# A two-layer encoder trunk on one core: queries through DRAM, fillers in one stream, other buffers and a vector-engine end

## The chip, the core and the metric

The kernel runs on one core of one Trainium2 chip. The metric is device time in microseconds (us); the median of several runs is compared. Engines: TensorE (PE, its weight loads are PEld), VectorE (DVE), ScalarE (ACT), GpSimd (POOL) and SyncE (SP, which here only issues DMAs).

## The reference

x is 1024 tokens of 1024 channels, mem 256 tokens. Two layers share one form:

```
mem_n = layer_norm(mem)
layer A: u, qm, gate = split(x @ a_w_in, [3072, 512, 2048])
         y_mix = silu(layer_norm(depthwise causal conv, 31 taps, 1536 channels, of (a * sigmoid(g))))
layer B: q, k, v, qi, ki, wi, qm, gate = split(x @ b_w_in, [1536, 128, 128, 512, 64, 8, 512, 2048])
         score = sum over 8 index heads of w * relu(qi . ki); the top 256 admissible keys per token are kept
         y_mix = 12-head attention with one key/value head over those keys, logits - slope * distance
both:    y_mem = 4-head attention of qm over mem_n
         x = layer_norm(4 ** 0.25 * x + (concat(y_mix, y_mem) * silu(gate)) @ w_out)
```

Everything is float32.

## The kernel before, in words

Every product is made of three matmuls on rounded halves: an operand is split into a high part (a copy to fp32r, usually by ACT) and a low part (operand minus high, by DVE or POOL), and hi*hi, hi*lo and lo*hi are summed in PSUM (`project_steps`, L143 to L154, one matmul per step of the generator, 24 for 128 output columns of 512 tokens; `project` runs them through). `load_cols` (L135) fetches the weights of 128 columns with two DMAs on SP and splits them, ACT the high and POOL the low part, or POOL both with `pool_only`. `split_ps` (L167) splits a PSUM result.

The program is written in one order; a planner simulates it and lays out each engine's own queue, which then runs strictly in order. `tc.high_priority(offset=...)` moves work forward or (`low`) back in that order, and `tc.issue_after(ins)` ties matmuls behind an instruction.

**Layer A.** x is loaded in 8 token tiles and transposed on PE into xhi and xlo (`transpose_in`, L238: eight transposes into a two-bank PSUM accumulator of tag acc, of which there are two, then `split_ps`). `rows_load` and `rows_in` (L250 to L264) bring conv weights and norm vectors as rows and transpose them into `chan`. Twelve channel blocks of the conv are made in pairs: `u_pair` (L384) projects gate and value, and `conv_pair` (L414) runs 30 multiply-adds over time shifts on DVE (L429) for each block, in a PSUM accumulator; ACT makes the first step (L419) and copies column 0 at the end (L428). `conv_stat` (L433) subtracts a common shift (the mean of block 0, by PE) and sums d and its square for the norm. DVE's conv runs at low priority beside PE's projections. In between stand `mem_prep` (L270, the memory tokens' norm and transposes, tile mf of tag mp), `head_a` (memory heads: `mem_k`, `mem_v`, `mem_q`, `mem_scores`, `mem_values`), `gate_a`, and `k_b`, `v_b` (layer B's memory keys and values, stored to DRAM). Tag mp has one buffer and is shared by mf, the softmax tile pn and kr. Then the output products (`out_group`, L585) and the norm (`layer_norm`, L195: statistics on DVE, scale on ACT, product with g on POOL, sum with b on DVE).

**Layer B.** *Index stage* (L786 to L806): for each of six token blocks and eight index heads PE makes scores (L794, L795) in one of two PSUM buffers, ACT takes relu (L800), and DVE accumulates (L805). After each step, FILL[b] matmuls of a gate projection are put in as fillers; FREE_GATES gates are used so. *Threshold stage*: DVE and ACT search for each token's 256th largest score bit by bit (`threshold`, L835), then `select` (L896) turns scores into a mask plus distance, on DVE at low priority. Beside it PE runs the remaining gates (`gate_steps`, to DRAM) and the queries of the first two heads (`head_q`, L814: high part by ACT, low part by DVE from PSUM, L824). *Attention* (L1096 to L1109): the sequence is heads 0, 1, memory head 0, heads 2, 3, 4, memory head 1 and so on, 16 in all. A head has four units of two token blocks: `scores` (L951; DVE maximum and subtraction, ACT exponential, POOL scale) and, one unit later, `values` (L981; PE transposes, split, products). `between` puts SHARE fillers after each group of transposes: the query of the next head or memory head, then one late gate; what is left runs at the head's end (L1106). Weights of the fillers are loaded one head ahead. The filler's PSUM tag pj has one buffer here.

**End.** `out_group` four times, the last in token order with `finish_b` (L1131): blocks 0 to 5 by `layer_norm` (block 5 with the last sum on POOL), blocks 6 and 7 by `layer_norm_late` (L201: statistics, L204 and two L207 on DVE, two stores).

Of the kernel before, what the change touches and what calls it, by code (L numbers as in the profile page):

```python
# [64 lines left out]
def trunk(ctx, tc, x, mem, mem_g, mem_b, a_w_in, conv_w, conv_b, ln_g, ln_b,  # L65
# [109 lines left out]
    def ln_moments(src):  # L175

        n = uid()
        st = small.tile([P, 2, 6], F32, tag="bnst", name=f"bnst{n}")
        for i in range(2):
            nc.vector.bn_stats(st[:, i, :], src[:, i * 512:(i + 1) * 512])  # L180
# [20 lines left out]
    def layer_norm_late(dst, src, g, b, o):  # L201

        mean, rs = ln_moments(src)
# [11 lines left out]
    with ExitStack() as actx:  # L215
# [28 lines left out]

        def x_in(t):
            transpose_in(xn[t], t)
# [23 lines left out]
        def mem_prep():  # L270
# [19 lines left out]
        def mem_k(w, h, kv=None, raw=None):  # L290

            pc = load_cols(w, h * P)
            o = psum()
            project(pc, mhi, mlo, 0, NMEM, o[:, :NMEM])
            if raw is None:
                split_ps(kv[:, 0:256], kv[:, 512:768], o[:, :NMEM])
            else:
                nc.scalar.activation(raw[:, 0:256], o[:, :NMEM], AF.Copy)

        def mem_v(w, h, kv=None, raw=None):  # L300
# [11 lines left out]
            else:  # L312
                nc.scalar.activation(raw[:, 256:512], o[:, :NMEM], AF.Copy)
# [20 lines left out]
        def mem_scores(pl, tags, q, kv, hf, banks_s):  # L334
# [4 lines left out]
            pn = pl.tile([P, 4, NMEM], F32, tag=tags["p"][hf], bufs=1, name=f"mp{n}")  # L339
# [18 lines left out]
            for i in range(4):  # L358
                nc.gpsimd.tensor_scalar(pn[:, i, :], pn[:, i, :], sm[:, i:i + 1], 1.0, op0=OP.mult, op1=OP.mult)
# [24 lines left out]
        def u_pair(i, start=False):  # L384
# [29 lines left out]
        def conv_pair(hs, i0):  # L414

            accs = []
            for i, h in zip((i0, i0 + 1), hs):
                acc = psb.tile([P, T], F32, tag="acc", bufs=2, name=f"acc{i}")
                nc.scalar.activation(acc, h, AF.Identity, bias=chan[:, i, TAPS:TAPS + 1], scale=chan[:, i, TAPS - 1:TAPS])  # L419
                accs.append(acc)  # L420
            for s in range(TAPS - 1, 0, -1):
                for i, h, acc in zip((i0, i0 + 1), hs, accs):
                    w = chan[:, i, TAPS - 1 - s:TAPS - s]
                    if s > 1:
                        dst = acc
                    else:
                        conv_out[i] = dst = co_tile(f"co{i}")
                        nc.scalar.activation(dst[:, 0:1], acc[:, 0:1], AF.Copy)  # L428
                    nc.vector.scalar_tensor_tensor(dst[:, s:], h[:, :T - s], w, acc[:, s:], op0=OP.mult, op1=OP.add)  # L429
# [3 lines left out]
        def conv_stat(i):  # L433

            d = conv_out[i]
            if i == 0:
                o = psb.tile([P, T], F32, tag="acc", bufs=2, name="cmean")
                for hf in range(2):
                    hs = slice(hf * 512, (hf + 1) * 512)
                    nc.tensor.matmul(o[:, hs], ones, d[:, hs], start=True, stop=True)  # L440
                    nc.scalar.activation(c_sh[:, hs], o[:, hs], AF.Copy, scale=1.0 / P)
            nc.gpsimd.tensor_tensor(d, d, c_sh, op=OP.subtract)
            if i == 0:
                nc.scalar.activation(sumd, d, AF.Copy)
                nc.scalar.activation(sumsq, d, AF.Square)
            else:
                sq = hp.tile([P, T], F32, tag="sq", bufs=1, name=f"sq{i}")
                nc.scalar.activation(sq, d, AF.Square)
                nc.gpsimd.tensor_tensor(sumd, sumd, d, op=OP.add)
# [9 lines left out]
        TA = {"q": ("mqh", "mql", 1), "p": ("mp", "mp"), "ph": ("mph", "mph"), "pl": ("mpl", "mpl")}  # L459
# [14 lines left out]
        kr = [None] * MEM_HEADS  # L474

        def k_b(h):
            kr[h] = am.tile([P, 512], F32, tag="mp", bufs=1, name=f"kvr{h}")
            mem_k(b_w_mkv, h, raw=kr[h])
# [703 lines left out]
```

## Time and profile before

| what | value |
|---|---|
| median of 3 runs | 1702.32 us (1701.68 to 1703.47) |
| profiled execution, its own time | 1699.66 us |
| its span, first to last instruction | 1697.8 us |
| PE busy | 1647.7 us, 97%, 8214 matmuls |
| DVE, ACT, POOL busy | 1148.6, 748.3, 668.7 us |
| first work of PE | 4.19 us after the span's start |
| index, threshold, attention stage | 859.5 to 914.3, to 1103.2, to 1511.6 us |

All times in the profile are from the span's start, of one profiled execution, which took 2.66 us less than the median. Matmuls overlap and their ends are modelled, so a busy time of PE is not work at its peak rate; start-to-start intervals tell more.

### The profile page before, as it was taken

What the parts mean: (1) busy time and instruction counts of PE and PEld (TensorE: products, weight loads), DVE (VectorE), ACT (ScalarE), POOL (GpSimd) and SP (SyncE); (2) the same over time, 40 slices, a digit from 0 to 9 for tenths busy, and PEclk for the clock granted to TensorE, in tenths of its full rate; (3) what the DMA queues carried; (4) which work ended last, traced back from release to release, by engine and by line L of the source; (5) the groups of instructions that cost most, each with busy time, mean ns of one, the idle gap of its engine ahead of it and who ended that gap; (6) DMA issues with size and microseconds to landing.
All of it is one profiled execution on the core that took longest, in us unless ns stands there. A gap on an engine that the chain in (4) does not pass through costs nothing.

```text
span 1697.8 us, 22413 instructions
## 1 busy us (share of the span) xinstructions
PE 1647.7 (97%) x8214; PEld 1380.4 (81%) x8214; DVE 1148.6 (68%) x1798; ACT 748.3 (44%) x1395; POOL 668.7 (39%) x577
## 2 busy tenths in 40 slices
PE   8999999999989999999989999899999999999997
PEld 6877888888878788888867877688888889888886
DVE  3799999989997565256168999765455555535337
ACT  4333344444343542124466776154454544533221
POOL 2344554635556366234322332133232323332233
PEclk9999999999999999999999999899999999999999
DMA  5121212222234553122311323212122121246212
GB/s 190 46 58 66 87 51 87 63 75 63 87 124 148 206 167 131 47 79 103 84 44 51 97 83 99 82 50 69 51 75 63 61 64 50 69 163 235 87 44 99
DMA packets 137789, 152.69 MB, mean 90 GB/s; under 512 B 7946, under 2 KB 108298, under 8 KB 137680
## 3 DMA queue, kind: packets, MB, share of 16 engines
q1 hardware_dynamic: 137680, 151.27, 27.9%
q8 instruction: 64, 1.05, 0.3%
q14 instruction: 45, 0.37, 0.1%
HBM read 112.71 MB, written 36.70 MB: 88 GB/s over the span
## 4 chain that ended last, share of the span: by engine, by line
PE 52%; DVE 12%; ACT 3%; issue 2%; DMA 1%; POOL 1%; DVEq 0%; ACTq 0%; SPq 0%; POOLq 0%
PE pj L149 7%; PE pj L151 7%; PE pj L153 7%; PE pj L601 5%; PE pj L600 5%; PE pj L599 5%; DVE junk L846 4%; PE pt L995 2%; DVE xs L805 2%; PE pt L600 2%; PE pt L599 2%; PE pt L601 2%; PE S L965 1%; PE S L967 1%; PE S L966 1%
## 5 line engine op out<-in xcount | busy, mean ns | idle before, releaser
L149 PE MATMUL pj<-xhi,wh 128*128 128x512 f32 (+2 forms) x1328 | 523.4, 394 | 13.8 <-DVE ql L824 7.2
L153 PE MATMUL pj<-xhi,wl 128*128 128x512 f32 (+2 forms) x1328 | 521.6, 393 | 0.0
L151 PE MATMUL pj<-xlo,wh 128*128 128x512 f32 (+2 forms) x1328 | 520.7, 392 | 0.2 <-DVE xlo L169 0.2
L132 POOL TENSOR_TENSOR wl<-wr,wh 128x512 fp32r<-128x512 f32 x258 | 340.4, 1326 | 437.9 <-ACT wh L131 420.1
L429 DVE SCALAR_TENSOR_TENSOR acc<-h,chan,acc 128x996 f32<-128x996 f32 (+27 forms) x348 | 418.5, 1263 | 16.1 <-ACT acc L419 14.7
L149 PEld LDWEIGHTS pj<-xhi,wh 128*128 128x128 f32 (+1 forms) x1328 | 250.7, 189 | 67.3 <-DVE ql L824 7.4
L153 PEld LDWEIGHTS pj<-xhi,wl 128*128 128x128 f32 (+1 forms) x1328 | 250.6, 189 | 49.8 <-issue 0.5
L151 PEld LDWEIGHTS pj<-xlo,wh 128*128 128x128 f32 (+1 forms) x1328 | 250.8, 189 | 48.6 <-DVE xlo L169 1.0
L131 ACT ACTIVATE wh<-wr 128x512 fp32r<-128x512 f32 (+1 forms) x230 | 143.8, 629 | 317.5 <-PE pj L151 162.7
L975 POOL TENSOR_SCALAR t<-t,smB 128x128 f32<-128x128 f32 (+3 forms) x96 | 72.0, 751 | 183.5 <-DVE smB L974 95.3
L600 PE MATMUL pj<-wl,xhi 128*128 128x512 f32 x320 | 124.1, 390 | 0.0
L599 PE MATMUL pj<-wh,xhi 128*128 128x512 f32 x320 | 123.5, 391 | 0.4 <-ACT xhi L559 0.3
L601 PE MATMUL pj<-wh,xlo 128*128 128x512 f32 x320 | 122.6, 390 | 0.0
L970 DVE CUSTOM_DVE_ANT_0 t<-S,xs 128x128 f32<-128x128 f32 (+3 forms) x96 | 70.9, 755 | 74.2 <-PE S L967 49.9
L169 DVE TENSOR_TENSOR pl<-pt,ph 128x512 fp32r<-128x512 f32 (+1 forms) x120 | 69.2, 580 | 59.4 <-ACT ph L168 58.5
L168 ACT ACTIVATE ph<-pt 128x512 fp32r<-128x512 f32 (+1 forms) x120 | 60.3, 509 | 77.5 <-PE pt L995 70.6
L973 ACT ACTIVATE t<-t,mxB 128x128 f32<-128x128 f32 (+3 forms) x96 | 74.1, 774 | 45.4 <-DVE mxB L972 45.3
L852 ACT ACTIVATE junka<-xs,cand 128x896 bf16<-128x896 f32 (+2 forms) x93 | 80.3, 864 | 29.3 <-DVE cand L877 23.0
L846 DVE TENSOR_SCALAR_CACHE_REDUCE junk<-xs,cand 128x1024 bf16<-128x1024 f32 (+2 forms) x93 | 89.9, 967 | 2.2
L599 PEld LDWEIGHTS pj<-wh,xhi 128*128 128x128 f32 x320 | 60.1, 188 | 14.0 <-ACT xhi L559 1.2
L601 PEld LDWEIGHTS pj<-wh,xlo 128*128 128x128 f32 x320 | 60.0, 188 | 13.0
L600 PEld LDWEIGHTS pj<-wl,xhi 128*128 128x128 f32 x320 | 60.1, 188 | 12.9
(296 smaller groups left out, 2792.9 us busy)
## 6 DMA issues: line engine op xcount, KB each, us to landing
wr<-in_a_w_in_dram SPq DMA_DIRECT2D x88, 256.0 KB
wr<-in_b_w_in_dram SPq DMA_DIRECT2D x76, 256.0 KB
wr<-in_a_w_out_dram SPq DMA_DIRECT2D x32, 256.0 KB
wr<-in_b_w_out_dram SPq DMA_DIRECT2D x32, 256.0 KB
yraw<-yb SPq DMA_DIRECT2D x16, 512.0 KB
gb<-gB SPq DMA_DIRECT2D x15, 512.0 KB
yb<-yB SPq DMA_DIRECT2D x12, 512.0 KB
sgB<-gb SPq DMA_DIRECT2D x11, 512.0 KB
```

Of the source, the lines that this page charges most:

```text
L131: nc.scalar.activation(hi, raw, AF.Copy)
L132: nc.gpsimd.tensor_tensor(lo, raw, hi.bitcast(F32), op=OP.subtract)
L149: nc.tensor.matmul(o, wh, xh, start=(k == 0), stop=False)
L151: nc.tensor.matmul(o, wh, xl, start=False, stop=False)
L153: nc.tensor.matmul(o, wl, xh, start=False, stop=(k == KD - 1))
L429: nc.vector.scalar_tensor_tensor(dst[:, s:], h[:, :T - s], w, acc[:, s:], op0=OP.mult, op1=OP.add)
L599: nc.tensor.matmul(o, yh[:, k, tsl], wh, start=(k == 0), stop=False)
L600: nc.tensor.matmul(o, yh[:, k, tsl], wl, start=False, stop=False)
L601: nc.tensor.matmul(o, yl[:, k, tsl], wh, start=False, stop=(k == 3))
L846: nc.vector.tensor_scalar(j[:, :nk(b)], xs(b), th[:, i:i + 1], None, op0=op, op1=OP.add, accum_out=c[:, i:i + 1])
L852: nc.scalar.activation(j[:, :nk(b)], xs(b), AF.Sign, bias=th[:, i:i + 1], scale=-(2.0 ** 24), accum_out=c[:, i:i + 1])
L973: nc.scalar.activation(t, t, AF.Exp, bias=mx[:, e:e + 1], scale=s, accum_out=sm[:, e:e + 1])
```

## The change

1. The start: nine transposes of the identity (`wake`) before x is there; tiles 2, 3 and 6 of x are transposed in two halves through one-bank PSUM tiles; tiles 4 to 7 come after the first projection; the rows of conv weights are loaded and transposed with the second channel block.
2. Conv: ACT's first step writes the output tile, shift 1 goes from it to the PSUM accumulator, shift 2 comes last and writes the output; the copy of column 0 goes, one DVE step on one column comes. The shift's mean uses the transposes' banks; sumd is no longer started by a copy.
3. Memory heads of layer A: mp has two buffers, kr one of its own, its two halves are stored apart, and the softmax scale is ACT's.
4. Fillers: two gates in the index stage with two fillers a step, gates 10 and 11 late. Queries 2 and up no longer go from PSUM to SBUF: ACT copies them raw, they are stored to DRAM (`spill`), three beside the threshold search and 11 as fillers of attention in one continuous `stream`, and read back and split one head ahead (`fetch`). The two early queries get their low part by POOL.
5. The end: block 5 by `layer_norm_late` too, the last product group in two pieces of 256 columns, block 7's statistics in three pieces.

```diff
-AHEAD = 1
-SHARE = (4, 8, 4)
-FREE_GATES = 1
+SHARE = (4, 8)
+FREE_GATES = 2
+SPILL = 3
-FILL = {7: 1, 6: 1, 5: 1, 4: 1, 3: 1, 2: 1}
-LATE_GATES = (11,)
+FILL = {7: 2, 6: 2, 5: 2, 4: 2, 3: 2, 2: 2}
+LATE_GATES = (10, 11)
...
         def x_in(t):
-            transpose_in(xn[t], t)
+            if t in (2, 3, 6):
+                transpose_halves(xn[t], t, psum if t == 2 else psum_t)
+            else:
+                transpose_in(xn[t], t)
+
+        def wake():
+            o = psum_t()
+            for k in range(9):
+                nc.tensor.transpose(o[:, k % 4 * P:(k % 4 + 1) * P], ident, ident)
...
-                mf = am.tile([P, 2, NMEM], F32, tag="mp", bufs=1, name=f"mf{g}")
+                mf = am.tile([P, 2, NMEM], F32, tag="mp", bufs=2, name=f"mf{g}")
...
             for i in range(4):
-                nc.gpsimd.tensor_scalar(pn[:, i, :], pn[:, i, :], sm[:, i:i + 1], 1.0, op0=OP.mult, op1=OP.mult)
+                if tags["p"][2] == 2:
+                    nc.scalar.activation(pn[:, i, :], pn[:, i, :], AF.Copy, scale=sm[:, i:i + 1])
+                else:
+                    nc.gpsimd.tensor_scalar(pn[:, i, :], pn[:, i, :], sm[:, i:i + 1], 1.0, op0=OP.mult, op1=OP.mult)
...
+            if i == 1:
                 rows_load()
             for hf in range(2):
-                if start and hf == 1:
+                og = psum()
+                project(pg, xhi, xlo, hf * 512, 512, og)
+                if start and hf == 0:
                     for t in range(4, NB):
                         x_in(t)
+                if i == 1 and hf == 0:
                     rows_in()
-                og = psum()
-                project(pg, xhi, xlo, hf * 512, 512, og)
...
+            for i, h in zip(pair, hs):
+                conv_out[i] = co_tile(f"co{i}")
+                nc.scalar.activation(conv_out[i], h, AF.Identity, bias=chan[:, i, TAPS:TAPS + 1],
+                                     scale=chan[:, i, TAPS - 1:TAPS])
+            for s in (1, *range(TAPS - 1, 1, -1)):
+                for i, h, acc in zip(pair, hs, accs):
+                    w = chan[:, i, TAPS - 1 - s:TAPS - s]
+                    src, dst = (conv_out[i] if s == 1 else acc), (conv_out[i] if s == 2 else acc)
+                    nc.vector.scalar_tensor_tensor(dst[:, s:], h[:, :T - s], w, src[:, s:], op0=OP.mult, op1=OP.add)
+                    if s == 1:
+                        nc.vector.scalar_tensor_tensor(src[:, 1:2], h[:, 0:1], w, src[:, 1:2], op0=OP.mult, op1=OP.add)
...
+                if early:
+                    raw = bq.tile([P, 512], F32, tag="qr", bufs=1, name=f"qr{h}_{hf}")
+                    nc.scalar.activation(raw, o, AF.Copy, scale=c)
+                    nc.gpsimd.tensor_tensor(ql[:, hs], raw, qh[:, hs].bitcast(F32), op=OP.subtract)
+                    continue
...
+        def raw_steps(c0, dst, pc, scale=1.0):
+            for hf in range(2):
+                o = psum()
+                yield from project_steps(pc, xhi, xlo, hf * 512, 512, o)
+                raw = bq.tile([P, 512], F32, tag="qr", bufs=1, name=f"qr{uid()}")
+                nc.scalar.activation(raw, o, AF.Copy, scale=scale)
+                nc.sync.dma_start(dst[:, hf * 512:(hf + 1) * 512], raw)
+
+        def spill(h, pool_only=False):
+            c0 = h * P if h < ATT_HEADS else B_QM + (h - ATT_HEADS) * P
+            pc = load_cols(b_w_in, c0, pool_only=pool_only)
+            yield
+            yield from raw_steps(c0, q_d[h], pc, SCALE / SLOPES[h] if h < ATT_HEADS else 1.0)
+
+        def fetch(h):
+            qh = bq.tile([P, T], F32R, tag="qh", bufs=2, name=f"qh{h}")
+            ql = bq.tile([P, T], F32R, tag="ql", bufs=2, name=f"ql{h}")
+            raw = ql.bitcast(F32)
+            nc.sync.dma_start(raw, q_d[h])
+            nc.scalar.activation(qh, raw, AF.Copy)
+            nc.gpsimd.tensor_tensor(ql, raw, qh.bitcast(F32), op=OP.subtract)
             queries[h] = (qh, ql)
...
+            for h in line[EARLY_Q:EARLY_Q + SPILL]:
+                run(spill(h, POOL_W))
             for h in range(EARLY_Q):
-                run(head_q(h, load_cols(b_w_in, h * P)))
+                run(head_q(h, load_cols(b_w_in, h * P), True))
...
+            def stream():
+                todo = [spill(h) for h in line[EARLY_Q + SPILL:]] + [late_gate(i) for i in LATE_GATES]
+                for k, steps in enumerate(todo):
+                    if k == 0:
+                        next(steps)
+                    if k + 1 < len(todo):
+                        next(todo[k + 1])
+                    yield from steps
...
             for i, (h, _, units) in enumerate(seq):
-                fill = ahead[i]() if ahead[i] else iter(())
-                share = SHARE[2 if i + 1 == len(seq) else h >= ATT_HEADS]
-                ahead[i + AHEAD] = filler(i + AHEAD)
+                share = SHARE[h >= ATT_HEADS]
+                if EARLY_Q <= i + 1 < len(seq):
+                    fetch(line[i + 1])
...
                     if j == len(units) - 1 and i + 1 < len(seq):
-                        run(fill)
                         seq[i + 1][1]()
...
-            if t < NB - 2:
+            if t < NB - 3:
                 z = bo.tile([P, T], F32, tag="z", bufs=2, name=f"zB{t}")
-                layer_norm(z, acc[t], gt, bt, nc.gpsimd if t == NB - 3 else None)
+                layer_norm(z, acc[t], gt, bt)
                 nc.sync.dma_start(o, z)
             else:
                 with tc.high_priority(offset=300):
-                    layer_norm_late(acc[t], acc[t], gt, bt, o)
+                    layer_norm_late(acc[t], acc[t], gt, bt, o, (0, 512, 768, 1024) if t == NB - 1 else (0, 512, 1024))
```

`line` is the sequence of the 16 heads and memory heads, `q_d` their DRAM tiles; `out_group` takes `halved=(1, NB - 1)` in its last call and makes that group in two pieces.

## Rows read from the trace of the kernel before

**Rows 1.** The page, part 1: the span, and each engine's busy time, share of the span and number of instructions.

```profile
span 1697.8 us, 22413 instructions
...
PE 1647.7 (97%) x8214; PEld 1380.4 (81%) x8214; DVE 1148.6 (68%) x1798; ACT 748.3 (44%) x1395; POOL 668.7 (39%) x577
```

**Rows 2.** Busy time by stretches (us from the span's start): start and end, length, then for PE, PEld, DVE, ACT and POOL the busy time and number of instructions, the granted share of TensorE's clock, the share of the DMA engines and GB/s. The index stage, the threshold stage, attention, a dense stretch of the last products, and three short ones.

```profile
859.50:914.30 54.80, 48.55 (x208) 34.25 (x207) 44.30 (x48) 39.66 (x53) 9.18 (x11) 1.00 0.09 22
914.30:1103.20 188.90, 179.93 (x775) 146.29 (x775) 168.35 (x372) 113.14 (x236) 58.34 (x72) 0.97 0.31 91
1103.20:1511.60 408.40, 402.95 (x2461) 358.64 (x2460) 218.54 (x616) 208.69 (x506) 135.42 (x164) 1.00 0.20 62
1600.00:1650.00 50.00, 50.00 (x222) 41.19 (x221) 18.87 (x25) 13.53 (x19) 19.14 (x14) 1.00 0.28 89
...
34.00:37.00 3.00, 2.78 (x7) 1.96 (x7) 2.50 (x5) 0.00 (x0) 0.00 (x0) 0.51 0.39 149
126.00:137.00 11.00, 7.27 (x20) 5.00 (x19) 7.61 (x7) 10.89 (x16) 8.56 (x5) 0.69 0.45 168
487.00:495.00 8.00, 4.64 (x24) 4.14 (x23) 8.00 (x10) 4.05 (x8) 3.34 (x7) 0.79 0.38 131
```

**Rows 3.** PE's waits over the whole run, longest total first, cut to three: engine, tile and line, what it waited for, us in total, times, longest.

```profile
PE pj L149 <- DVE ql L824: 7.2, 1, 7.2
...
PE pj L149 <- ACT ga L321: 4.7, 2, 3.4
...
PE pt L285 <- ACT co L428: 2.4, 1, 2.4
```

**Rows 4.** The same list for attention alone (1103 to 1512), its first row.

```profile
PE pv L1006 <- ACT ph L168: 3.7, 4, 0.9
```

**Rows 5.** Index stage. First, of the score tile's instructions, the matmuls of line 794 (min/median/max ns, first and last start, shapes); then one of them in the timeline, with its wait; then DVE's accumulation of line 805.

```profile
L794 PE MATMUL S<-khh,qs x80: 304/397/505, 850.7 to 913.5; 128*128 128x512 f32 x24, 128*128 128x384 f32 x24, 128*128 128x448 f32 x16, 128*128 128x320 f32 x16
...
870.91 0.51 PE L794 MATMUL S<-khh,qs 128*128 128x512 f32 x1 [1.71 <-ACT relu L800]
...
L805 DVE SCALAR_TENSOR_TENSOR xs<-relu,win,xs x42: 617/1018/1721, 863.9 to 916.7; 128x1024 f32<-128x1024 f32 x7, 128x896 f32<-128x896 f32 x7, 128x384 f32<-128x384 f32 x7, 128x768 f32<-128x768 f32 x7
```

**Rows 6.** Timeline at the end of the threshold stage: start us, us, engine, line, operation, tiles, and in brackets the idle time before it and what ended it. PE's first matmul after its wait, and two instructions of DVE.

```profile
1089.19 0.80 PE L149 MATMUL pj<-xhi,wh 128*128 128x512 f32 x1 [7.20 <-DVE ql L824]
...
1088.45 0.68 DVE L824 SCALAR_TENSOR_TENSOR ql<-pj,qh 128x512 fp32r<-128x512 f32 x1
...
1090.23 1.09 DVE L919 SCALAR_TENSOR_TENSOR xs<-eq,xs 128x896 f32<-128x896 f32 x1
```

**Rows 7.** What a round trip over DRAM is made of. The longest single wait of SP's queue in attention; the existing ACT copy and POOL subtraction of a 128x1024 tile that comes back from DRAM (us in all, mean ns); and a transfer of such a tile, from the chain that ended last (start us, us).

```profile
SPq L1019 <- DVE yB L1017: 59.7, 4, 26.7
...
L559 ACT ACTIVATE xhi<-yraw 128x1024 fp32r<-128x1024 f32 x2 | 2.1, 1059 | 1.8 <-DMA yraw<-yb 1.2 <-PE pj L153 0.6
...
L560 POOL TENSOR_TENSOR xlo<-yraw,xhi 128x1024 fp32r<-128x1024 f32 x2 | 4.8, 2404 | 3.9 <-ACT xhi L559 3.9
...
1517.90 4.76 DMA yraw<-yb
```

**Rows 8.** Timeline of the start: the last step of making the identity tile on POOL, PE's first work, a projection matmul before and one after the clock rises, and three that waited.

```profile
1.76 0.29 POOL masks.py:199 TENSOR_SCALAR_AFFINE_SELECT ident<-ident 128x128 f32<-128x128 f32 x1
...
4.19 3.65 PE L242 MATMUL px<-ident,xn 128*128 128x128 f32 x16 [4.19 <-DMA xn<-in_x_dram]
...
15.04 0.63 PE L151 MATMUL pj<-xlo,wh 128*128 128x512 f32 x1
...
16.86 0.40 PE L149 MATMUL pj<-xhi,wh 128*128 128x512 f32 x1
...
25.33 0.50 PE L149 MATMUL pj<-xhi,wh 128*128 128x512 f32 x1 [0.78 <-ACT wh L131]
...
31.09 1.09 PE L242 MATMUL px<-ident,xn 128*128 128x128 f32 x8 [0.53 <-DVE xlo L169]
33.30 1.04 PE L149 MATMUL pj<-xhi,wh 128*128 128x512 f32 x2 [1.11 <-ACT xhi L168]
```

**Rows 9.** Timeline of ACT between 126 and 132: the first step of a conv block and the one-column copy.

```profile
127.30 1.21 ACT L419 ACTIVATE acc<-h,chan 128x1024 f32<-128x1024 f32 x1
...
128.90 0.16 ACT L428 ACTIVATE co<-acc 128x1 f32<-128x1 f32 x1
```

**Rows 10.** Timeline of PE between 487 and 499: the two matmuls that waited.

```profile
491.33 0.58 PE L149 MATMUL pj<-mhi,wh 128*128 128x256 f32 x1 [3.36 <-ACT ga L321]
...
497.99 0.39 PE L149 MATMUL pj<-mhi,wh 128*128 128x256 f32 x1 [1.34 <-ACT kvr L298]
```

**Rows 11.** Timeline of the end: PE's last matmul, POOL's last instruction, and four of DVE.

```profile
1687.76 0.40 PE L601 MATMUL pj<-wh,xlo 128*128 128x512 f32 x1
...
1685.16 3.25 POOL L199 TENSOR_TENSOR zB<-zB,btB 128x1024 f32<-128x1024 f32 x1
...
1686.75 2.88 DVE L207 SCALAR_TENSOR_TENSOR accB<-accB,bnrs,btB 128x512 f32<-128x512 f32 x2
...
1690.15 0.67 DVE L606 TENSOR_TENSOR accB<-pj,accB 128x512 f32<-128x512 f32 x1
...
1691.83 1.28 DVE L204 SCALAR_TENSOR_TENSOR accB<-accB,bnmv,gtB 128x1024 f32<-128x1024 f32 x1
...
1693.22 1.41 DVE L207 SCALAR_TENSOR_TENSOR accB<-accB,bnrs,btB 128x512 f32<-128x512 f32 x2
```

More of the change, by code (lines that the diff above doesn't have):

```diff
@@ L173, in split_sb, with ln_moments @@
         nc.gpsimd.tensor_tensor(lo, src, hi.bitcast(F32), op=OP.subtract)
-    def ln_moments(src):
+    def ln_moments(src, cuts=(0, 512, 1024)):
         n = uid()
-        st = small.tile([P, 2, 6], F32, tag="bnst", name=f"bnst{n}")
-        for i in range(2):
-            nc.vector.bn_stats(st[:, i, :], src[:, i * 512:(i + 1) * 512])
+        st = small.tile([P, 4, 6], F32, tag="bnst", name=f"bnst{n}")[:, :len(cuts) - 1, :]
+        for i, (c, e) in enumerate(zip(cuts, cuts[1:])):
+            nc.vector.bn_stats(st[:, i, :], src[:, c:e])
         mv = small.tile([P, 2], F32, tag="bnmv", name=f"bnmv{n}")
@@ L414, in conv_pair @@
         def conv_pair(hs, i0):
[L416 to L422, printed above, removed]
-                    w = chan[:, i, TAPS - 1 - s:TAPS - s]
[L424 to L429, printed above, removed]
+            pair = (i0, i0 + 1)
+            accs = [psb.tile([P, T], F32, tag="acc", bufs=2, name=f"acc{i}") for i in pair]
+            for i, h in zip(pair, hs):
[4 more added lines that the diff above has]
+                for i, h, acc in zip(pair, hs, accs):
+                    w = chan[:, i, TAPS - 1 - s:TAPS - s]
+                    src, dst = (conv_out[i] if s == 1 else acc), (conv_out[i] if s == 2 else acc)
+                    nc.vector.scalar_tensor_tensor(dst[:, s:], h[:, :T - s], w, src[:, s:], op0=OP.mult, op1=OP.add)
+                    if s == 1:
+                        nc.vector.scalar_tensor_tensor(src[:, 1:2], h[:, 0:1], w, src[:, 1:2], op0=OP.mult, op1=OP.add)
             for i in (i0, i0 + 1):
@@ L436, in conv_stat @@
             if i == 0:
-                o = psb.tile([P, T], F32, tag="acc", bufs=2, name="cmean")
                 for hf in range(2):
                     hs = slice(hf * 512, (hf + 1) * 512)
-                    nc.tensor.matmul(o[:, hs], ones, d[:, hs], start=True, stop=True)
-                    nc.scalar.activation(c_sh[:, hs], o[:, hs], AF.Copy, scale=1.0 / P)
+                    o = psum_t()
+                    nc.tensor.matmul(o, ones, d[:, hs], start=True, stop=True)
+                    nc.scalar.activation(c_sh[:, hs], o, AF.Copy, scale=1.0 / P)
             nc.gpsimd.tensor_tensor(d, d, c_sh, op=OP.subtract)
             if i == 0:
-                nc.scalar.activation(sumd, d, AF.Copy)
                 nc.scalar.activation(sumsq, d, AF.Square)
@@ L448, in conv_stat @@
                 nc.scalar.activation(sq, d, AF.Square)
-                nc.gpsimd.tensor_tensor(sumd, sumd, d, op=OP.add)
+                nc.gpsimd.tensor_tensor(sumd, conv_out[0] if i == 1 else sumd, d, op=OP.add)
                 nc.gpsimd.tensor_tensor(sumsq, sumsq, sq, op=OP.add)
@@ L499, in u_conv @@
                 conv_pair(hs, i)
+        wake()
         for t in range(4):
@@ L1088, in between @@
                         next(fill, None)
-            ahead = {i: filler(i) for i in range(AHEAD)}
+            next(fill)
             seq[0][1]()
```

92 lines of the change are left out of this document (46 added, 46 removed).

## The prediction

> **What bounds the kernel now.** I read the page first: TensorE (PE) is busy 1647.7 us of a span of 1697.8 us, the others 39 to 68% [rows 1]. So time comes only out of stretches in which PE does not run at its dense rate, or out of the two ends. Next I cut the span into stages [rows 2]. The dense stretch at 1600 to 1650 us is the yardstick: 222 matmuls of 512 columns in 50.0 us, 0.225 us each. One *unit* below is a projection of 128 columns of weights over all 1024 tokens: 8 slices x 3 matmuls x 2 halves = 48 matmuls, 10.8 us. There are 32 units in the second layer (12 head queries, 4 memory queries, 16 gates), and the change moves them about. Before, 1 lies in the index stage (859.5 to 914.3), 16 in the threshold stage (914.3 to 1103.2), 15 in attention (1103.2 to 1511.6). Third, PE's waits over the whole run [rows 3], and those in attention alone [rows 4]: there the longest total is 3.7 us in 408.4 us. Attention is bound by PE; every unit taken out of it is worth nearly 10.8 us. The reader is to see that idle PE time is not spread evenly: it sits in the start, at 126 to 137, at 487 to 495, in the index stage and at 1081 to 1095.
>
> **The change, part by part.**
>
> *Units moved.* FREE_GATES 2 with FILL 2 puts 2 units into the index stage. Threshold then holds 12 gates, 3 spilled queries and 2 early ones, 17 units. Attention keeps 11 spilled queries and 2 late gates, 13 units.
>
> Index stage, 54.8 us: its scores are 160 matmuls; the 80 of one line have 24 x 512, 24 x 384, 16 x 448 and 16 x 320 columns, 422 on average [rows 5], so 160 x 422/512 x 0.225 = 29.7 us at the dense rate. With 48 fillers (10.8) that is 40.5 us, 14.3 us less than the stage takes. Scores wait for ACT's relu (1.71 us in the row shown), and that runs in step with VectorE's (DVE) accumulation, 1.02 us a step in the median [rows 5]. With 96 fillers PE needs 51.3 us, still under 54.8. But for the widest block PE then needs 4 x 0.225 + 2 x 0.225 = 1.35 us a step, about what DVE takes there, so the two will at times wait for each other. Bounds: +0 (all in idle time) to +10.8 (none). I take +2.5, near the low end, as the count of starts is the nearer row. The busy row would tell otherwise: 48.55 of 54.8 us busy leaves 6.25 us of room, and the stage would grow by 4.6. The Trainium skill (Perfetto Trace Analysis, section Identifying the Most-Contended Engine) says that matmul busy time is a poor measure, since matmuls are pipelined, and to go by LDWEIGHTS busy instead. By that, 34.25 of 54.8 us is 62%, against 41.19 of 50 (82%) in the dense stretch: about a quarter of the stage is free, 13 us, and the growth would be 0; the trace's count of starts sides with the page.
>
> Threshold stage, 188.9 us: 16 units are 172.8 us. PE waits 7.2 us, until 1089.19, for `ql` of L824, a DVE instruction that sits in DVE's queue behind select (it runs at 1088.45; select steps still follow, the last at 1090.23) [rows 3, 6]. Then the clock is at its lower level of 1.2 GHz for some time (mean granted 0.97 of the stage, 0.03 x 188.9 = 5.7 us lost). With `early`, `ql` is made by POOL from an SBUF copy, so PE no longer waits for select. 17 units are 183.6 us, ending about 5 us below 188.9; I leave 4 us for waits like the present ones and take -1. Select ends near 1091 now [rows 6]; moved by +2.5 it still ends before PE's 17 units do (914.3 + 2.5 + 183.6 = 1100), so nobody waits for it: that is the cover, and it is 7 us thick. If it goes, the old wait of 7 us is back. Bounds -5 to +7.
>
> Attention: -2 units = -21.6 us. Per unit two DVE subtractions go (they cost PE nothing), and a round trip over DRAM comes: 28 writes of 256 KB and 14 reads of 512 KB on SP's queue, an ACT copy of 1.06 us and a POOL subtraction of 2.40 us per query, a DMA of 4.76 us if nothing else runs [rows 7]. A head lasts 408.4/16 = 25.5 us and `fetch` is issued one head ahead: 4.76 + 1.06 + 2.40 = 8.2 us fit three times. What is queued behind: ACT's exponentials and PSUM copies behind the copy of `fetch`, if its DMA is late. Also the 8 fillers left over at each head's end, which covered the last softmax, are gone, as all 640 filler slots now interleave 624. Bounds: 0 to +10 us of new waits; I take +2, near the waits there are [rows 4]. Net -19.6.
>
> Sum of the moved units: +2.5 - 1 - 19.6 = **-18.1 us** (bounds -27 to 0).
>
> *Start.* Nine dummy transposes run from about 2 us, when the identity tile is there, until x lands at 4.19 us [rows 8], so PE's work starts 2.1 us earlier. The first projections run at the lower clock (0.63 us against 0.40 us at 16.86) [rows 8]; if the clock rises as long after the first work as now, the stretch from 14.4 to 16.5 is at full rate: -1.0. The tables of the conv weights move out of the start to the second channel block (10 small DMAs on SP behind the x loads and weights, a POOL memset, 12 transposes, so the conv begins somewhat later, on DVE and off PE's path), tiles 2, 3 and 6 are transposed in halves through other banks, and tiles 4 to 7 come before the second projection. Waits of 0.78, 0.53 and 1.11 us [rows 8] and 3 us at a granted 0.51 (1.5 us) [rows 2] are what this can take: 3.9 us; I take all of it, and nothing for other waits on x. **-5** (bounds -1 to -7).
>
> *126 to 137 us.* 11.0 - 7.27 = 3.7 us idle and 0.31 x 11 = 3.4 us of lower clock [rows 2]. PE waits there for ACT (L428 2.4 us) [rows 3], and ACT's queue holds the first conv steps, L419 1.21 us and the copy L428 that waits for DVE [rows 9]; L428 goes, the initial step no longer waits for a PSUM accumulator, the copy into sumd goes, and mf is double-buffered. The mean now needs two turns of the transposes' banks, which may wait instead. **-5** of 7.1 (bounds +1 to -7).
>
> *487 to 495 us.* PE waits 3.36 us for a Silu behind an exponential and then 1.34 us for kvr [rows 10], with 1.7 us of lower clock (0.21 x 8) [rows 2]: 6.4. kr gets its own buffer, mp a second one, and the softmax scale goes from POOL to ACT. The Silu may still be behind an exponential that waits for DVE. **-4** (bounds 0 to -6.4).
>
> *End.* The last matmul is issued at 1687.76, but DVE adds its result only at 1690.15, held by two multiplications that take 2.88 us while POOL adds, against 1.41 us afterwards [rows 11]. With block 5 on DVE, POOL is empty, so the steps are short; the last add and its moments work on 256 columns (about half of 0.67 us saved). Block 5 puts 1.28 + 1.41 us more on DVE just before. **-1.5** (bounds 0 to -3); 24 matmuls of 256 columns for 12 of 512 cost nothing visible.
>
> *No price:* a second late gate (an ACT Silu and a DVE product more, beside dense matmuls), 12 single-column conv steps on DVE, the split of the kv stores. If PE did wait for these, it is 1 to 3 us.
>
> Sum: -18.1 - 5 - 5 - 4 - 1.5 = **-33.6 us**. The profiled run took 1699.66 us (span 1697.8), 2.66 below the median of 1702.32. 1699.66 - 33.6 + 2.66 = **1668.7 us**.
>
> **The rivals.**
>
> *The moved work is half eaten.* The index stage grows by the 10.8 us, or attention pays 10 us for the lost cover. For: relu and DVE already pace the index stage. Against: 14 us of room. The move gives -6 instead of -18.1: 1681 us.
>
> *The round trip blocks ACT (slower).* SP takes its queue in order and in attention has waits of up to 26.7 us on one instruction [rows 7], about a head. A `fetch` behind one comes a head late; the copy then stops ACT, hence exponentials, hence PE. All of 8.2 us exposed on 14 queries is 115 us, half of it 57 us, 1726 us. It decides from 33.6/14 = 2.4 us per query on. Against: SP's waits are waits for work that is not ready, placed by a planner that knows the order.
>
> *Everything returns.* Each engine's order is laid anew; new waits take the place of those at 126 and 487, and the move is eaten: 1700 us, no change.
>
> *Every bound at its good end:* -27 - 7 - 7 - 6.4 - 3 = -50: 1652 us.
>
> **How the numbers follow.** Forecast 0.60, half eaten 0.20, all good 0.07, blocked 0.09, everything returns 0.04. About 0.2% (3.4 us) can be told from no change. Faster: 0.60 + 0.20 + 0.07 = 0.87; same 0.04; slower 0.09. The range 1650 to 1690 holds the forecast, most of the half-eaten case and the good ends.
>
> **What would show it.** Right: attention near 389 us without new PE waits, the index stage under 58 us, no wait on ql at its end, granted clock without a dip at 1085 and 129. Wrong: PE waiting in attention for qh or for ACT behind a DMA of q; an index stage of 65 us; threshold ending later than 1105.

## The result and the profile after

The changed kernel takes 1673.98 us (median; 1672.74 to 1674.50), the kernel before, beside it on the same chip, 1702.00 (1700.84 to 1703.47): a ratio of 0.9839, interval 0.9825 to 0.9852, so 28 us faster. The forecast was 1668.7 us with a range of 1650 to 1690: right in direction and range, 5.3 us too low. The two profiled executions took 1699.66 and 1674.50 us, spans of 1697.8 and 1672.7. The tables below go by these, where 25.1 us went.

The page's first part, as [rows 1]:

```profile
span 1672.7 us, 22575 instructions
...
PE 1637.0 (98%) x8235; PEld 1376.5 (82%) x8235; DVE 1142.6 (68%) x1786; ACT 776.1 (46%) x1435; POOL 697.8 (42%) x563
```

Cut at the same events of PE before and after (a projection matmul is counted when it has 512 columns, and a stretch ends where the named one ends):

| stretch | before, us | after, us | difference | forecast |
|---|---|---|---|---|
| start to the 385th projection matmul | 112.6 | 109.5 | -3.1 | -5 |
| to the 481st (most of the memory's preparation) | 32.1 | 35.6 | +3.5 | -5 |
| to the 1441st | 258.1 | 256.3 | -1.8 | 0 |
| to the 1801st (holds 487 to 495) | 123.7 | 119.1 | -4.6 | -4 |
| to the index stage | 333.0 | 333.4 | +0.4 | 0 |
| index stage | 54.8 | 56.8 | +2.0 | +2.5 |
| threshold stage | 189.0 | 189.9 | +0.9 | -1 |
| attention | 408.3 | 388.9 | -19.4 | -19.6 |
| last products, tail | 186.2 | 183.2 | -3.0 | -1.5 |
| sum | 1697.8 | 1672.7 | -25.1 | -33.6 |

Each column is one execution. In the runs below, kernels in which PE and SP start with the same instructions in the same order reach the 385th projection between 109.4 and 112.0 us, so the first difference is uncertain by some 2 us. The second isn't: the five of these runs (e1, e6, e7, e8, e10) that leave the memory's preparation as in the changed kernel take 34.8 to 35.9 us there, and e2, which leaves it as before, takes 31.5.

The same stages as busy time by stretches (columns as in [rows 2]): index, threshold, attention, the dense stretch, then three short ones.

```profile
853.90:910.70 56.80, 54.00 (x255) 44.44 (x254) 47.32 (x49) 40.91 (x55) 12.31 (x14) 1.00 0.15 40
910.70:1100.60 189.90, 187.84 (x820) 152.79 (x820) 163.95 (x365) 114.65 (x236) 66.37 (x78) 1.00 0.33 96
1100.60:1489.50 388.90, 384.31 (x2367) 339.69 (x2367) 201.78 (x591) 220.16 (x518) 170.11 (x178) 1.00 0.31 101
1600.00:1650.00 50.00, 50.00 (x222) 41.40 (x221) 25.70 (x48) 11.45 (x16) 18.58 (x11) 1.00 0.15 57
27.10:30.50 3.40, 3.40 (x9) 2.65 (x8) 1.37 (x2) 3.39 (x6) 1.99 (x2) 0.50 0.53 148
126.00:137.00 11.00, 6.89 (x18) 4.93 (x19) 11.00 (x11) 7.49 (x11) 4.38 (x4) 0.53 0.22 90
482.00:490.00 8.00, 8.00 (x50) 7.17 (x49) 8.00 (x10) 4.03 (x9) 5.78 (x4) 1.00 0.11 33
```

Three things are to be seen here. The index stage holds 255 matmul records where it held 208, for 2 us more. The threshold stage has no lower clock left (1.00, it was 0.97) and 820 records for 775, in the same time. And 126 to 137 us, which was to be mended, has become worse: the granted clock is 0.53 where it was 0.69, near the 1.2 GHz level.

PE's waits over the whole run, the three longest; then the first of attention alone, as [rows 3, 4]:

```profile
PE pj L149 <- ACT ga L340: 4.1, 4, 1.7
PE pt L304 <- ACT mf L305: 3.5, 4, 2.0
PE S L820 <- ACT relu L826: 2.7, 5, 0.8
```

```profile
PE S L1030 <- ACT mp L374: 0.9, 2, 0.6
```

The 7.2 us for `ql` are gone, as are the 3.36 for one Silu (the longest is now 1.7). New is `mf`: PE's transposes of the memory wait for ACT to empty their bank.

The round trip, as [rows 7]: SP's longest wait in attention, ACT's copy and POOL's subtraction of a fetched query, and the transfers on the chain that ended last.

```profile
SPq L871 <- ACT qr L870: 110.5, 19, 13.3
...
L886 ACT ACTIVATE qh<-ql 128x1024 fp32r<-128x1024 f32 x14 | 14.9, 1061 | 11.5 <-DMA ql<-qd 11.5
...
L887 POOL TENSOR_TENSOR ql<-ql,qh 128x1024 fp32r<-128x1024 f32 x14 | 33.6, 2403 | 11.2 <-ACT qh L886 10.6 <-PE pt L1060 0.4
...
1111.68 3.17 DMA ql<-qd
1139.12 4.98 DMA ql<-qd
...
1335.24 3.84 DMA ql<-qd
```

ACT did stop in front of the copy, 11.5 us in 10 of 14 cases, which is the mechanism of the slower rival; but no wait of PE in attention comes from `qh` or `ql`. The fetch a whole head ahead covers it.

### The profile page after: what moved, and what is told of

It reads as the page before. It is cut to its first block, busy times and chain, and to the rows that moved or that the text cites. A ratio compares the mean times of both kernels' runs of the same rounds, so it can differ in the third digit from the quotient of the medians.

```text
span 1672.7 us, 22575 instructions
## 1 busy us (share of the span) xinstructions
PE 1637.0 (98%) x8235; PEld 1376.5 (82%) x8235; DVE 1142.6 (68%) x1786; ACT 776.1 (46%) x1435; POOL 697.8 (42%) x563
## 4 chain that ended last, share of the span: by engine, by line
PE 70%; DVE 13%; ACT 5%; issue 4%; DMA 4%; POOL 2%; SPq 1%; DVEq 0%; ACTq 0%; POOLq 0%
PE pj L149 14%; PE pj L151 13%; PE pj L153 13%; DVE acc L451 4%; PE pj L627 4%; PE pj L625 4%; PE pj L626 4%; DVE junk L909 3%; PE pt L1060 2%; ACT junka L915 2%; DMA wr<-in_a_w_out_dram 1%; PE S L1030 1%; PE S L1031 1%; PE S L1032 1%; PE pv L1072 1%
## 5 line engine op out<-in xcount | busy, mean ns | idle before, releaser
L132 POOL TENSOR_TENSOR wl<-wr,wh 128x512 fp32r<-128x512 f32 x258 | 347.3, 1353 | 435.2 <-ACT wh L131 425.5
L451 DVE SCALAR_TENSOR_TENSOR acc<-h,chan,acc 128x1004 f32<-128x1004 f32 (+26 forms) x336 | 403.4, 1264 | 0.6
L1040 POOL TENSOR_SCALAR t<-t,smB 128x128 f32<-128x128 f32 (+4 forms) x96 | 72.0, 752 | 126.4 <-DVE smB L1039 81.9
L626 PE MATMUL pj<-wl,xhi 128*128 128x512 f32 (+1 forms) x324 | 124.5, 386 | 0.0
L627 PE MATMUL pj<-wh,xlo 128*128 128x512 f32 (+1 forms) x324 | 124.5, 386 | 0.0
L625 PE MATMUL pj<-wh,xhi 128*128 128x512 f32 (+1 forms) x324 | 123.2, 386 | 0.0
L1035 DVE CUSTOM_DVE_ANT_0 t<-S,xs 128x128 f32<-128x128 f32 (+4 forms) x96 | 71.5, 755 | 46.4 <-PE S L1032 34.2
L1038 ACT ACTIVATE t<-t,mxB 128x128 f32<-128x128 f32 (+4 forms) x96 | 74.3, 775 | 37.5 <-DVE mxB L1037 36.8
```

The lines of the kernel that those rows point to most:

```text
L132: nc.gpsimd.tensor_tensor(lo, raw, hi.bitcast(F32), op=OP.subtract)
L625: nc.tensor.matmul(o, yh[:, k, tsl], wh[:, c:e], start=(k == 0), stop=False)
L626: nc.tensor.matmul(o, yh[:, k, tsl], wl[:, c:e], start=False, stop=False)
L627: nc.tensor.matmul(o, yl[:, k, tsl], wh[:, c:e], start=False, stop=(k == 3))
L1038: nc.scalar.activation(t, t, AF.Exp, bias=mx[:, e:e + 1], scale=s, accum_out=sm[:, e:e + 1])
```

## The experiments

Each was timed against the kernel before on the same chip. The two halves of the change come first.

**e1: everything but the moved units.** The second layer from its index stage to attention as before, with DVE's early queries; the first layer and the end as changed.

```
-SHARE = (4, 8)
-FREE_GATES = 2
-SPILL = 3
+AHEAD = 1
+SHARE = (4, 8, 4)
+FREE_GATES = 1
...
-FILL = {7: 2, 6: 2, 5: 2, 4: 2, 3: 2, 2: 2}
-LATE_GATES = (10, 11)
+FILL = {7: 1, 6: 1, 5: 1, 4: 1, 3: 1, 2: 1}
+LATE_GATES = (11,)
...
```

What is left out puts back the fillers of attention and DVE's early queries.

> The changed kernel with layer B's fillers as before (1 gate in the index stage, queries split straight from PSUM by DVE, one late gate); layer A and the end stay changed. Theory (the moved units bring about two thirds): 1002 to 1004 of 1000 parts less than the kernel before, that is 8 to 11 us below 1702, about 1692. Rival (the gain lies in layer A and the ends, attention gives little): about 20 us below, 1682. Second rival (only the whole works, as each engine's order is laid anew): no gain, 1702.

Measured: 1689.31 us, ratio 0.9919 (0.9906 to 0.9933). Index, threshold and attention stages are back at 54.8, 187.9 and 408.6 us, and so is the wait:

```profile
1082.57 0.79 PE L149 MATMUL pj<-xhi,wh 128*128 128x512 f32 x1 [7.20 <-DVE ql L850]
```

**e2: the moved units alone.** The counterpart: that part of the second layer as changed, all else as before.

> The kernel before with layer B's fillers alone changed. Theory: 16 to 19 us below the kernel before, about 1685, with attention some 20 us shorter, the index stage 2 us longer and no wait on ql. Rival: 8 us below, 1694.

Measured: 1686.39 us, ratio 0.9901 (0.9886 to 0.9916); stages of 56.9, 189.9 and 389.4 us. Against the kernel before (1702.47), e1 gains 13.2 us and e2 16.1, together 29.2 for the 28 of the whole change: the halves add, and the gain is a little more than half moved work.

**e7: the second index filler taken back.** One unit in the index stage, so 18 in the threshold stage.

```
-FREE_GATES = 2
-FILL = {7: 2, 6: 2, 5: 2, 4: 2, 3: 2, 2: 2}
+FREE_GATES = 1
+FILL = {7: 1, 6: 1, 5: 1, 4: 1, 3: 1, 2: 1}
```

> The changed kernel with one filler a step and one gate in the index stage; the threshold stage gets 18 units. Theory (the second unit costs the index stage 2 us of its 10.9 and PE bounds the threshold stage): index stage back at 54.8 us, threshold stage 10.9 us longer, 9 us slower than the changed kernel, 1683. Rival (the units in the index stage delay DVE's search, which bounds the threshold stage): same, 1674.

Measured: 1681.80 us, ratio 0.9880 (0.9860 to 0.9901), about 8 us more than the changed kernel. Its index and threshold stages:

```profile
853.30:908.00 54.70, 48.67 (x208) 34.09 (x207) 44.26 (x48) 39.58 (x53) 9.20 (x11) 1.00 0.09 22
908.00:1108.10 200.10, 198.27 (x870) 161.95 (x869) 163.99 (x365) 115.72 (x240) 70.33 (x82) 1.00 0.33 97
```

The unit costs 2.1 us in the index stage (56.8 against 54.7) and 10.2 us in the threshold stage (200.1 against 189.9). PE's busy time in the index stage, 48.67 us, looks like 6 us of room, yet 48 more matmuls, 10.8 us of work, cost only 2.1. The count of starts, which leaves 14.3 us of room, came a little nearer, though it alone says 0.

**e6: the early queries' low part by the vector engine again,** one cause proposed for the `ql` wait's end.

```
-                run(head_q(h, load_cols(b_w_in, h * P), True))
+                run(head_q(h, load_cols(b_w_in, h * P)))
```

> The changed kernel with the low part of the two early queries made by DVE from PSUM again. Theory (with 17 units the early queries come after select has ended, 1085 us, so that nobody waits; the POOL detour is not what removed the wait): within 1 us of the changed kernel, 1674. Rival (the planner puts the subtraction behind select and the wait is back): 5 to 8 us slower, 1680.

Measured: 1673.70 us, ratio 0.9833 (0.9811 to 0.9856), not to be told from the changed kernel, and no wait for `ql` in the list. So POOL's detour isn't needed: with 17 units the first low part falls due just as select is done. ACT's copy for it ends at 1082.65 us, select's last step at 1083.18, and DVE begins the low part at 1083.10. Whether POOL's detour alone, with 16 units, would have been enough wasn't tried.

**e8: the end as before.**

> The changed kernel with the end as before (block 5 by the norm that also uses ACT and POOL, the last product group whole). Theory: from the last matmul to the end 9.6 us instead of 8.8, and the products 1 us longer: 1 to 2.5 us slower than the changed kernel, 1676. Rival (the end is bound by the stores): no change, 1674.

Measured: 1674.85 us, ratio 0.9843 (0.9821 to 0.9866). From PE's last matmul to the end it takes 9.8 us, against 8.8 in the changed kernel; the 0.9 us between the medians is within what the runs scatter. The stretch from attention's end to the last instruction tells more: 183.9 us here, 182.8 to 183.1 in all nine kernels with the new end, 186.0 before and 184.9 in e2 (counted from the end of attention's last product). So the end's edits bring 0.9 us of that stretch's gain, and the rest has another cause.

**e10: no dummy transposes at the start.**

```
-        wake()
         for t in range(4):
```

> The changed kernel without the nine transposes of the identity at the head of PE's queue; the output is the same. Theory (they bring the clock up before the first data arrive, and this makes most of the start's gain): the full clock comes 3 to 8 us later than at 6.6 us, the first projection 1 to 2 us later than at 12.2, and the time is 1 to 3 us longer: 1675 to 1677 us. Rival (the start is paced by the arrival of the first token blocks, and the gain comes from taking blocks 2, 3 and 6 in halves and from projecting before blocks 4 to 7): first projection within 0.5 us of 12.2, 1673.5 to 1674.5 us.

Measured: 1674.93 us, ratio 0.9853 (0.9839 to 0.9866). The theory's mechanism fell. PE starts on the first token block at 4.23 us, and the first projection runs at 10.95 us, not later than with them (12.18 in the changed kernel; 10.89 in e1 and 11.10 in e6, which start as it does). The matmuls that follow take 0.39 us each, the full clock's time, in both. The first projection waits for the token blocks and for ACT's split (`xhi`, 1.34 us here, 1.43 with them), so 2 us of earlier work on PE do not bring it forward. The time itself, 0.95 us above the changed kernel, lies between the two forecasts, and the intervals of the two ratios overlap: a gain of about 1 us from the dummy transposes is neither shown nor excluded.

**e4: the row loads later on SP's queue.** In the changed kernel the ten small loads of the conv tables have moved in the program to the second channel block, but the planner, which orders by what is ready, issued them in the start all the same, nine of the ten ahead of block 0's last weights. SP's issues (start us, us):

```profile
9.67 0.33 SPq L272 DMA_DIRECT2D rows<-in_a_conv_w_dram  x1
...
17.33 0.22 SPq L274 DMA_DIRECT2D rows<-in_a_ln_b_dram  x1
20.48 0.22 SPq L276 DMA_DIRECT2D rows<-in_mem_ln_g_dram  x1
20.80 0.41 SPq L122 DMA_DIRECT2D wr<-in_a_w_in_dram  x1
...
21.70 2.29 SPq L122 DMA_DIRECT2D wr<-in_a_w_in_dram  x2
```

SP's own waits show what makes this long (who waited for what, us in total, times, longest): before seven of these issues SP waits for loads of x and of weights to land, and before a later one for the rows themselves. All that time block 0's last weights stand behind them in the queue.

```profile
SPq L274 <- DMA xn<-in_x_dram: 3.0, 3, 1.1
SPq L276 <- DMA rows<-in_a_conv_w_dram: 2.9, 1, 2.9
...
SPq L274 <- DMA wr<-in_a_w_in_dram: 1.7, 3, 0.6
...
SPq L272 <- DMA xn<-in_x_dram: 1.1, 1, 1.1
```

On PE there are then two waits for the weights, after which the clock falls (0.63 us a matmul):

```profile
25.45 0.50 PE L149 MATMUL pj<-xhi,wh 128*128 128x512 f32 x1 [1.01 <-ACT wh L131]
...
26.80 0.59 PE L153 MATMUL pj<-xhi,wl 128*128 128x512 f32 x1 [0.62 <-POOL wl L132]
27.18 0.63 PE L149 MATMUL pj<-xhi,wh 128*128 128x512 f32 x1
```

The edit makes them issue behind block 1's weights:

```
...
-        nc.sync.dma_start(raw, src3)
+        lastw[0] = nc.sync.dma_start(raw, src3)
...
             if i == 1:
-                rows_load()
+                with tc.issue_after(lastw[0].ins):
+                    rows_load()
```

> The changed kernel with the ten loads of the conv rows queued on SP behind the last weights of the second channel block; the planner had issued them at 9.7 to 21 us all the same. Theory (they hold up the second weight tile of the first block, PE's wait of 1.0 us at 25.4 and the dip at 27): both go, 2 to 4 us below the changed kernel, about 1671. Rival (the weights wait for their buffer): no change, 1674; or slower by 2 us if the conv's start is late.

Measured: 1668.02 us, ratio 0.9793 (0.9778 to 0.9809), 6 us better than the changed kernel and more than the theory's 2 to 4. In its SP issues the five weight loads go first:

```profile
11.68 9.49 SPq L124 DMA_DIRECT2D wr<-in_a_w_in_dram  x5
21.22 0.40 SPq L274 DMA_DIRECT2D rows<-in_a_conv_w_dram  x1
```

No wait of PE shows in 22 to 34 us, its clock stays up, and the 385th projection ends at 103.8 us (109.5 in the changed kernel, 112.6 before).

**e3: the mean of conv block 0 in an accumulator's bank, as before.** Why did 126 to 137 us become worse? The PE timeline of the changed kernel (columns as in [rows 6]):

```profile
120.03 1.88 PE L464 MATMUL pt<-co,ones 128*128 128x512 f32 x4
121.75 0.43 PE L304 MATMUL pt<-ident,mt 128*128 128x128 f32 x2
122.60 0.89 PE L304 MATMUL pt<-ident,mt 128*128 128x128 f32 x4 [0.42 <-ACT c_sh L465]
...
127.26 0.69 PE L304 MATMUL pt<-ident,mt 128*128 128x128 f32 x2 [2.03 <-ACT mf L305]
129.06 0.69 PE L304 MATMUL pt<-ident,mt 128*128 128x128 f32 x2 [1.11 <-ACT mf L305]
```

The mean (L464) now takes the two banks of the transposes, and its place in the program is ahead of the memory's preparation. So all 16 transposes of the memory, whose data are ready at 65 us, wait until block 0's conv is done, and then come in one burst without a projection in between, paced by ACT. Before, four ran at 46 us; the other twelve ran from 112.0 to 129.3 us, done no sooner than now, but among 48 projection matmuls:

```profile
112.01 0.38 PE L285 MATMUL pt<-ident,mt 128*128 128x128 f32 x2
...
117.93 0.38 PE L285 MATMUL pt<-ident,mt 128*128 128x128 f32 x2
...
121.36 0.38 PE L285 MATMUL pt<-ident,mt 128*128 128x128 f32 x2
```

The edit of e3:

```
+                o = psb.tile([P, T], F32, tag="acc", bufs=2, name="cmean")
                 for hf in range(2):
...
-                    o = psum_t()
...
```

> The changed kernel with the conv's mean back in a PSUM accumulator of tag acc instead of two tiles of the transposes' banks. Theory (these two tiles come first in the rotation of the transposes' banks, so that all 16 transposes of the memory tokens wait for the first conv block and then come in one burst): the burst at 122 to 129 us goes, the dip of the granted clock at 126 goes, 5 to 9 us below the changed kernel, about 1666. Rival (ACT is full there anyway): within 2 us of the changed kernel, 1674.

Measured: 1678.22 us, ratio 0.9859 (0.9841 to 0.9876): 4 us slower than the changed kernel, though the burst is gone. Busy time at 100 to 150 us in the changed kernel, then in e3 (more PE records, full clock):

```profile
100.00:150.00 50.00, 44.27 (x182) 34.02 (x181) 50.00 (x45) 20.80 (x32) 23.66 (x17) 0.90 0.19 64
```

```profile
100.00:150.00 50.00, 48.51 (x216) 38.98 (x215) 46.08 (x37) 23.32 (x38) 29.24 (x18) 1.00 0.21 69
```

But the mean now holds an accumulator that the conv needs: the last tap of the conv ends at 551.8 us, not 542.6, and PE has new waits near 303 to 343 us, 1.8 us on DVE's `kva` the longest, and around 624 to 637.

**e5: e4 and e3 together.**

> The changed kernel with the mean in a PSUM accumulator and the rows' loads late. If the two add as measured (+4 and -6 against the changed kernel), 1672. Theory (the mean's place took the burst away, 8 us, and only a conv that started and ran later gave it back at 300 and 630 us; with the rows out of the way it starts on time): 1661 to 1664. Rival (the new waits belong to the mean in an accumulator): 1670 to 1674, with waits at 300 and 630 us again.

Measured: 1672.26 us, ratio 0.9827 (0.9804 to 0.9850), 4 us slower than e4 alone. The conv ends 9.6 us later than in e4 and the same waits come back, so they belong to the mean's place and not to the start.

**e9: e4, with the memory's preparation ahead of the mean.** The mean stays in the transposes' banks, but the memory takes them first.

```
             hs = [u_pair(i, start=i == 0), u_pair(i + 1)]
+            if i == 0:
+                with low(200):
+                    mem_prep()
             with low(50000):
                 conv_pair(hs, i)
 ...
         u_conv(2)
-        mem_prep()
```

> The kernel e4_rowslate (rows behind block 1's weights) with one more edit: the preparation of the memory takes its two-bank tiles ahead of conv block 0's mean, as it did before the change in effect, so that its 16 transposes need not wait for that conv. In the program's order the transposes spread again over some 70 projection matmuls, and half of the mean comes later, some 215 matmuls behind the other half. Theory (the burst of transposes at 122 to 130 us is what turned the expected -5 there into +3.5): the starts of PE in excess between 100 and 150 us fall by 5 to 8 us, no fall of the granted clock there, 1660 to 1664 us against 1668 of e4. Rival 1 (what is taken from the burst is given back, as when the mean lay in an accumulator bank): the late half of the mean holds up block 0's statistics and through them the conv, whose last tap ends 5 to 10 us later than e4's 534.6, with new waits of PE near 300 and 620 us: 1668 to 1673 us. Rival 2 (the burst costs nothing that the conv does not take later anyway): conv end unchanged, 1667 to 1669 us.

Measured: 1663.84 us (1662.55 to 1664.63), ratio 0.9784 (0.9770 to 0.9797), the fastest of all here, though its interval overlaps e4's. Each against its own kernel before, e9 leads e4 by 1.5 us (0.9784 and 0.9793), and the profiled executions lie 1.4 us apart (1664.63 and 1665.98), so the 4.2 us between the medians are not all its own. The burst is gone: 14 of the 16 transposes run from 102.0 to 116.6 us among 57 projections, without a wait. Busy time at 100 to 150 and at 440 to 500 us, first of e4, then of e9:

```profile
100.00:150.00 50.00, 44.27 (x185) 34.26 (x184) 50.00 (x44) 21.54 (x34) 26.09 (x19) 0.93 0.21 69
440.00:500.00 60.00, 58.87 (x322) 50.63 (x321) 60.00 (x63) 32.98 (x63) 33.16 (x22) 1.00 0.31 91
```

```profile
100.00:150.00 50.00, 48.71 (x218) 39.21 (x217) 50.00 (x44) 19.96 (x32) 20.12 (x16) 1.00 0.19 60
440.00:500.00 60.00, 57.01 (x311) 48.54 (x310) 59.25 (x58) 33.08 (x63) 34.21 (x22) 0.97 0.30 93
```

The 481st projection ends 7.7 us earlier than in e4 (130.8 against 138.5), but the 1801st only 1.5 us earlier (510.9 against 512.4), and the conv's end is 5.4 us later (540.0 against 534.6). Theory and first rival both hold in part: the burst costs about 7 us where it stands, and most of that is given back before the conv ends, in part at 440 to 500 us, where PE has 11 records fewer and the clock reads 0.97. Between these two projections PE's waits grow from 0.9 to 4.4 us; 3.8 of the 4.4 end with ACT, 0.6 with DVE.

## Why the prediction was right, and where its sizes were off

**Moved units: right.** -16.5 us of the forecast -18.1 (+2.0, +0.9, -19.4), and -16.1 with nothing else changed (e2). Index: +2.0 for the forecast +2.5, and e7 shows the 10.2 us that the unit would have cost elsewhere. The count of starts alone said 0, busy time 4.6; the 2.5 was an allowance near the count of starts, and its size isn't derived. PE's waits for the relu in that stage fell from 5.9 to 2.7 us: part of the new matmuls went into them. By the Trainium skill's reading (Perfetto Trace Analysis, Identifying the Most-Contended Engine) it was 0 as well; the trace shows +2.0.

**Threshold: right, for a reason that wasn't needed.** The prediction credited POOL's `ql` with the end of the 7.2 us wait. e6 shows that the wait stays away without it: the seventeenth unit keeps PE busy until select's end, the cover that the prediction named. It is not 7 us thick: that compares select with the end of all 17 units, but the first low part is due much earlier, in e6 0.4 us before DVE takes it. The stage came out 1.9 us longer than forecast: 17 units at 10.8 are 183.6, and 6.3 us remain, not the 4 left for waits. PE's waits are 2.1 of these (busy 187.84 of 189.90); the projections lie 0.229 us apart there, not 0.225.

**Attention: right** to 0.2 us, by luck in its smaller term. Two units less would be 386.7 us, and the 2.2 us above that look like the +2 taken for new waits. But PE did not idle more: 5.4 us before (402.95 busy of 408.40), 4.6 after (384.31 of 388.90). The 2.2 us lie in the busy time, and why isn't shown. ACT's waits for the fetch stayed under the cover.

**126 to 137 us: the step that failed,** +3.5 instead of -5, 8.5 us. That is as much as the whole difference between -25.1 and -33.6: the misses of the other terms (+1.6 moved units, +1.9 start, -1.8 at 145 to 402 us, -0.6, +0.4, -1.5 end) cancel, which is luck. The prediction removed the copy L428 as the wait's cause and noted in one sentence that the mean "now needs two turns of the transposes' banks, which may wait instead". L428's wait of 2.4 us is indeed gone. But that sentence held the answer, and its upper bound of +1, for which no working is given, was too small: not the mean waits, the transposes behind it do, and they run in one burst. From the 385th to the 481st projection PE's waits rise from 3.7 to 5.6 us (`mf` 3.5 of them), and the clock reads 0.50 for 10.2 us (126.1 to 136.3) instead of 6.8 (129.1 to 135.9); with half of the lower clock's time taken as lost, an estimate, that is 1.9 + 1.7 us, about the +3.5. The price of a bank taken by a late producer is that of everything behind it in the program's order, 16 transposes and their ACT copies, and a lower clock after it. e9 shows further that even the hoped-for gain would not have stayed: of 7.7 us won there, 1.5 were left at the 1801st projection. A likely reason, argued and not shown, is DVE: it is busy 468.90 of the 478 us from 52 to 530 in the changed kernel, so PE's lead there soon meets work of DVE.

**Start: mis-sized,** -3.1 for -5. One execution can't place it well (above): kernels with the new start reach the 385th projection at 109.4 to 112.0 us, those with the old one at 112.6 and, in e2, 112.0, so the gain is 0 to 3 us. The 2.1 us of earlier work bring the first projection no further forward (e10), and the table loads were taken as moved since the program moves them; SP still issued them at 9.7 to 21.3 us. Moved in fact (e4), the 385th projection gains 8.8 us on the kernel before, more than the term's bound of -7.

**487 to 495: right,** -4.6 for -4. Which of the three edits (kr's own buffer, the second mp buffer, ACT's softmax scale) did it was not separated. The waits left there are of about 1 us:

```profile
470.65 0.39 PE L149 MATMUL pj<-mhi,wh 128*128 128x256 f32 x1 [0.90 <-ACT ga L340]
```

**End:** -3.0 for -1.5. The long steps of 2.88 us [rows 11] take 1.40 with POOL at rest; in e8, where POOL adds beside them again (1659.82 to 1663.07), they take 2.87. The last product's sum now follows PE's last matmul at once, in two pieces:

```profile
1663.64 0.28 PE L627 MATMUL pj<-wh,xlo 128*128 128x256 f32 x1
...
1663.69 0.74 DVE L632 TENSOR_TENSOR accB<-pj,accB 128x256 f32<-128x256 f32 x2
1664.34 1.40 DVE L207 SCALAR_TENSOR_TENSOR accB<-accB,bnrs,btB 128x512 f32<-128x512 f32 x2
```

Of the -3.0 the tail itself is 0.8 (9.6 to 8.8), and e8 gives 0.9 for all the end's edits. The other 2 us are in the products, come from another part of the change, and their cause is open.

The rivals: the half-eaten case falls with the index stage's +2.0 and attention's -19.4, the blocked ACT by attention's list of waits. "Everything returns" was true of one place, the memory's preparation. Two sums of the prediction are off, without weight for the result: its own bounds of the moved units add up to +6.2 at the upper end (10.8 + 7 - 11.6), not 0, and half eaten is -9.8 or -10.1 by its two conditions (-1.8 with both), not -6.

Of the 5.3 us by which the forecast missed the median, the terms account for 8.4 (-25.16 between the profiled executions for -33.6); 3.2 come back, since the profiled execution of before lay 2.66 us below its median and that of after 0.52 above.

## What to carry to other kernels

To find the room for moved work, count an engine's starts beside its busy time (they said 0 and 4.6 us here, the trace 2.0), and move the work to where another engine sets the pace: one unit cost 2.1 us there and 10.2 in a dense stage. When a tile changes its bank, list who comes after it in that bank in the program's order: an early-ready user behind a late producer pays the whole wait. And an edit that moves a load in the program need not move it on the queue; read the queue's issue times after, and tie the load to a later instruction if it must be later.

## What the runs showed of the hardware that was not expected

The same eight small row loads were issued 0.85 to 1.3 us apart in the changed kernel (9.67 to 17.33 us) and 0.29 to 0.69 us apart, mostly 0.3, in e4 (21.22 to 23.90), at 0.22 to 0.40 us an issue both times. The difference is no price of a small load: 5.8 us of the 7.7 are the seven waits for loads of x and weights to land that are shown with e4; in e4 one such wait is left, of 0.4 us. The clock did not follow one wait alone: after waits of 1.01 and 0.62 us at 25 to 27 us it read 0.50 from 27.1 in the changed kernel, after waits of 2.04 and 0.62 us at the same place in e10 it still read 1.00 until 30.5, and 0.66 in the 3.5 us after. What made the difference is open.
